# Merging TensorE's streams by estimated queues of three engines in place of constants alone

## The chip, the cores and the metric

The kernel runs on one core of a Trainium2 chip. The metric is the device time of one execution in microseconds; a lower time is better. The core has TensorE (PE in the rows, its weight loads PEld), VectorE (DVE), ScalarE (ACT), GpSimd (POOL) and SyncE (SP), which issues transfers. All five run their own instructions in order and wait for one another by semaphores.

## The reference

One inference step of a decoder trunk of two layers (`DEPTH = 2`) in float32: width 1024, a prompt of 1024 positions, and eight sample sequences with one new position each and a state of their own. A layer is, cut to what matters:

```python
p   = x @ w_in                                # q, k, v for 8 heads; r, k, v and low-rank columns for RWKV
att = dilated_attention(rope(q), rope(k), v)  # 3 patterns (window, dilation), merged per position and head
att = att * rsqrt(mean(att ** 2)) * att_gain
rw, S_T = rwkv7_time_mix(token_shift(p_rwkv), wkv0)   # delta-rule state, group norm, bonus, gate
x1  = layer_norm(ALPHA * x + concat(att, rw) @ w_out)
y   = layer_norm(ALPHA * x1 + square(relu(x1 @ w_up)) @ w_down)
```

The results are `y` for prompt and samples, the last input rows, the RWKV states and the keys and values.

## The kernel before

**Tiles.** Activations stand transposed, the 1024 features on partitions in eight tiles and positions in columns. The prompt is worked in two halves `h` of 512 columns; the second half carries the eight samples. A dense product is done to nearly float32 accuracy with three passes of a reduced format: `x` and `w` are split into a high and a low part (`xh`, `xl`, `wh`, `wl`), and `dense_steps` issues three matmuls a tile (lines 390 to 392). `Weights.fill` loads a weight piece with a DMA on ScalarE's queue, casts it on ScalarE (line 363) and subtracts on VectorE (line 364), a few pieces ahead.

**Streams.** The order of TensorE's instructions is fixed when the program is built. Seven Python generators emit the program in pieces, each up to its next `yield`:

- `dense`, the main one: `in_proj` for a layer's half, then `half(l, h)`, which is the output projection, a first normalisation, the feed-forward part in eight groups `g`, and a second normalisation;
- `s1` and `s2`, the two stages of the RWKV recurrence in units of 256 columns; `norm`, its group norm and gate (`normed`, with matmuls `pgm` and `pgv`);
- `att` (`attention`: scores `pS`, exponentials in tiles `E`, transposes `pET`, products `po` and `pof`), `post` (transposed values) and `kv` (the samples' attention).

`Streams.run` merges them by a model of time, `now`. Each step of a generator yields four things:

```python
cost, hold, lat, s[3] = r          # s[3]: the bank that its next step takes
self.now += cost                   # TensorE's own time for this step
if hold:
    self.hist[hold[0]].append(self.now + hold[1] * self.slack(s))   # the bank is free again
s[2] = self.now + lat * self.slack(s)                               # the stream can go on
```

`lat` stands for the time that the other engines need before the stream's next matmuls have their operands, and `hold` for the time until a bank of PSUM has been read. Both are constants, multiplied for side streams by `SLK`, 1.2 in a stream's first phase and 2.2 later. `run` steps the first side stream whose time has come; where none is ready, the dense stream goes on, and where that is not ready either, `now` jumps to the earliest. Four kinds of banks are shared out: `d` (3) for dense tiles, `a` (2) for most side work, `r` (1) and `o` (2) for the recurrence. `after(key, lat=...)` makes a stream wait until another has noted a key.

The tile scheduler orders the instructions of the other engines by its own model; only TensorE keeps the order in which the pieces were emitted. A matmul that stands too early in that order waits for its operand, and everything behind it on TensorE waits too.

**Where dense waits.** `half(l, h)` begins when stage two, attention and (for the second half) the samples' streams of that half are done (`Mix.wait`). In the last layer's first half this wait stands ahead of the second normalisation, at `g == LNG` (line 1000), since the next half follows at once; then `LayerNorm.start` issues the statistics matmul `lnc` (line 731).

**Constants that the change touches.** `HOLD = (2400, 4500)` is the bank time of dense tiles in the two `passes` (`out2` and `down`), in which VectorE also works on a normalisation; elsewhere it is 900. In `normed`, 900 and 1800 are the latencies ahead of `pgm` (line 1420) and `pgv` (line 1432).

Of the kernel before, what the change touches and what calls it, by code (L numbers as in the profile page):

```python
# [45 lines left out]
        "dense": (561e3, 580e3, 413e3, 427e3)}  # L46
RUN = (1600, 3200)
SWITCH = 280
HOLD = (2400, 4500)
SLK = (1.2, 2.2)  # L50
PACE = 2.0
LEAD = 0.25
# [95 lines left out]
class Streams:  # L148
# [6 lines left out]

    def __init__(self, depth):
        self.now = 0.0
        self.depth = depth  # L160
        self.hist = {b: [] for b in depth}
        self.streams = []
        self.times = {}
        self.cost = {}
        self.phase = {}
        self.work = {}
        self.stay = 0.0
        self.away = False

    def add(self, name, gen, slack=(1.0, 1.0)):  # L170
        self.streams.append([name, gen, 0.0, None, None, slack])

    def slack(self, s):
        return s[5][self.phase.get(s[0], (0,))[0] > 0]

    def note(self, *key):
        self.times[key] = self.now
# [12 lines left out]
    def ahead(self, s):  # L190

        name, main = s[0], self.streams[-1][0]
        if name not in self.work or self.phase.get(name, (0,))[0] != self.phase.get(main, (-9,))[0] + 1:
            return False
        return self.share(name) > self.share(main) * PACE + LEAD
# [14 lines left out]

    def step(self, s):
        s[3] = s[4] = None
        try:
            r = next(s[1])
        except StopIteration:
            self.streams.remove(s)
            return
        if callable(r):
            s[4] = r
            return  # L220
        cost, hold, lat, s[3] = r
        self.now += cost
        self.cost[s[0]] = self.cost.get(s[0], 0.0) + cost
        if hold:
            self.hist[hold[0]].append(self.now + hold[1] * self.slack(s))
        s[2] = self.now + lat * self.slack(s)

    def run(self):
        while self.streams:
# [34 lines left out]
    return bass.AP(tensor=ap.tensor, offset=ap.offset, ap=[list(ap.ap[0])] + [list(d) for d in dims])  # L264


@with_exitstack
def body(ctx, tc, I, O):
    nc = tc.nc
    PE, V, A, G, S = nc.tensor, nc.vector, nc.scalar, nc.gpsimd, nc.sync  # L270
    AQ = G

    cp = ctx.enter_context(tc.tile_pool(name="cp", bufs=1))
    dr = ctx.enter_context(tc.tile_pool(name="dr", bufs=1, space=DRAM))
# [6 lines left out]

    BANKS = {"r": 1, "o": 2, "d": 3, "a": 2}
    R = Streams(BANKS)
    after, note = R.after, R.note

    def bank(tag, name):
# [48 lines left out]
    class Weights:  # L335
# [4 lines left out]
        def __init__(self, specs):  # L340
            self.pieces, self.first = [], []
            for srcs, m, dest in specs:
                self.first.append(len(self.pieces))
                self.pieces += [(src, m, dest) for src in srcs]
            self.first.append(len(self.pieces))
            self.out, self.copies = {}, []
            self.nl = self.i = self.kept = 0
# [48 lines left out]
        res += pts  # L396
        res.append(cost)

    def dense(items, kts, xhh, xll, evac, hold=900):

        res = []
        yield (0, None, 0, "d")
        yield from dense_steps(items, kts, xhh, xll, res)
        for it, p in zip(items, res):
            r = evac(it, p)
            if r is not None:
                yield r
        for i, it in enumerate(items):
            yield (res[-1] if i == 0 else 0, ("d", hold + 500 * i), 0, None)

    def cols(t):
        return lambda kt, c0, n: xc(t, kt, slice(c0, c0 + n))
# [92 lines left out]
    def pv(l, nm, i):  # L505
        a = PROWS[nm][0] + i
        return par[l][0][:, a:a + 1]
# [284 lines left out]
    def acc(hs):  # L792
        return (lambda kt, c0, n: hs[kt][0][:, c0:c0 + n]), (lambda kt, c0, n: hs[kt][1][:, c0:c0 + n])
# [73 lines left out]
    def half(l, h, prev=None):  # L867
# [5 lines left out]
        if over:  # L873
# [8 lines left out]
            t = None  # L882
# [67 lines left out]
        def out2(o, w, c0, nn):  # L950
            def ev(it, p):
                _, _, c0, n = it
                evs.append(V.tensor_tensor(src(o, c0, n), p[:, :n], src(o, c0, n), op=ALU.add))
            return dense([(w, 128, c0, nn)], K4, *acc(hs), ev, HOLD[c0 > 0])
        yield from passes(out2, ln)

        def up(w, pair, c0, nn):
# [67 lines left out]
        def down(o, w, c0, nn):  # L1025
            def ev(it, p):
                _, _, c0, n = it
                to = t[:, o, c0:c0 + n]
                evs.append(V.tensor_tensor(to, p[:, :n], to, op=ALU.add))  # L1029
            return dense([(w, 128, c0, nn)], K4, *acc(hs), ev, HOLD[c0 > 0])  # L1030
        yield from passes(down, ln)

        def store(c0, n):
# [72 lines left out]
    def stage1(l, h, p, u, s, lw, out):  # L1106
# [107 lines left out]
        for hd in range(2):  # L1214
            for c in range(2):
# [2 lines left out]
                                pbs[hd].rearrange("p (b c x) -> p c b x", c=2, x=128)[:, c],  # L1218
                                bc(C("si")[:, o:o + 1], [(0, 2), (1, 128)]), op=ALU.mult)
        yield (0, ("a", 1100), 0, None)  # L1220
        d1, d2, d3 = d_el[s % 2]
        LBp = LB.rearrange("p h (b c) x -> p c (h b) x", c=2)
        for c in range(2):
# [23 lines left out]
            S.dma_start(XT[64 * c:64 * c + 64], drows(d3, c))  # L1247
        bp = tmp("sq")[:, :n]
        V.scalar_tensor_tensor(bp, zr, pv(l, "rk", p), f, op0=ALU.mult, op1=ALU.mult)
        yield (460, ("a", 1900), 0, "a")  # L1250
        tx = R.now + 30000
        pb = bank("a", "pt1")
# [162 lines left out]
    def normed(l, h, p, u, s, gup, gs):  # L1415

        y, bv = ys.pop(s)
        yield (0, None, 900, "o")
        pb = bank("o", "pgm")
        PE.matmul(pb[:, 0:256], C("blk"), y, start=True, stop=True)  # L1420
        PE.matmul(pb[:, 256:512], gup, gs[:, 0:256], start=True, stop=True)
# [2 lines left out]
        A.copy(gg, pb[:, 256:512])  # L1424
        sq = rq.tile([128, 4, 128], F32, tag="FG", name="gq").rearrange("p a b -> p (a b)")[:, 0:256]
        A.activation(sq, y, AF.Square)
        yield (860, ("o", 1000), 1800, "o")
        pb = bank("o", "pgv")
        if h == 1 and u == NU - 1:
            PE.matmul(pb[:, 256:256 + NB], gup, gs[:, UN:UN + NB], start=True, stop=True)  # L1430
# [149 lines left out]
    def attention(l, h, p, ops, vT, ahead):  # L1580
# [5 lines left out]
        for j in range(4):  # L1586
# [29 lines left out]
            for hd in range(2):  # L1616
# [13 lines left out]
                V.reciprocal(mx[:, 8 + hd:9 + hd], mx[:, 6 + hd:7 + hd])  # L1630
                V.tensor_scalar(E[:, :f + w], E[:, :f + w], mx[:, 8 + hd:9 + hd], None, op0=ALU.mult)
            if j == 3:
                ahead()
            yield (0, None, ALT0 + (f + w) * ALT1, "a")
            if h == 1 and j % 2 == 0:
                FT = ap_.tile([128, 2, 4, 2, 32], F32, tag="FT", name="FT")
# [277 lines left out]
```

## Time and profile before

| | |
|---|---|
| median of 3 runs | 3244.0 us (3242.94 to 3245.74) |
| profiled execution, its own time | 3244.69 us |
| its span, first to last instruction | 3242.9 us |
| TensorE matmuls busy | 3054.3 us, 94% |
| VectorE, ScalarE, GpSimd busy | 63%, 44%, 29% |
| mean granted TensorE clock | 0.974 of full |

The busy times are those of one profiled execution; idle time of TensorE is the span less its busy time. A matmul's end is modelled, so a busy TensorE is not one at its peak. In a list of waits, `PE pgm L1420 <- ACT y L1401` says that TensorE sat idle before the matmul into `pgm` of line 1420 until ScalarE's instruction on `y` of line 1401 had ended.

### The profile page before, as it was taken

How to read it: one execution, taken by the hardware profiler on the slowest of the kernel's cores; microseconds unless marked ns; L12 is line 12 of the kernel's file. 1: busy time of each engine (PE TensorE's matmuls, PEld its weight loads, DVE VectorE, ACT ScalarE, POOL GpSimd, SP SyncE). 2: the span in 40 equal slices, each digit the busy share in tenths (PEclk: the TensorE clock that was granted, in tenths of full speed). 3: DMA queues.
4: the chain of work that ended last, by engine and by line, in shares of the span. 5: the costliest groups of instructions: out<-in, count | busy, mean ns of one | idle time of the engine just before them, and what ended most of it. 6: DMA issues, size and time to landing. Idle time of an engine off the chain costs nothing. (4 is left out here: it accounts for less than half of the span.)

```text
span 3242.9 us, 66797 instructions
## 1 busy us (share of the span) xinstructions
PE 3054.3 (94%) x25212; PEld 2651.7 (82%) x25212; DVE 2034.9 (63%) x4671; ACT 1439.2 (44%) x3266; POOL 930.1 (29%) x1761
## 2 busy tenths in 40 slices
PE   9999999899989999989999999888999999899998
PEld 6778887777767887778899999877777777889997
DVE  5666666865575575677565566467755754965556
ACT  4446444453433363455443345344543333543333
POOL 1444435532310214453310112545242201400011
PEclk9999999999999999989999999999999999999999
DMA  7445455344343355533233236544343433422332
GB/s 233 144 128 143 132 144 164 88 129 122 105 134 103 98 157 156 163 101 105 85 91 97 89 94 183 142 134 124 104 131 108 121 123 105 137 81 93 93 91 82
DMA packets 370506, 393.64 MB, mean 121 GB/s; under 512 B 145816, under 2 KB 223080, under 8 KB 370184
## 3 DMA queue, kind: packets, MB, share of 16 engines
q10 hardware_dynamic: 121152, 213.44, 22.0%
q1 hardware_dynamic: 249032, 175.93, 19.1%
q8 instruction: 199, 3.26, 0.4%
q14 instruction: 123, 1.01, 0.1%
HBM read 325.30 MB, written 63.97 MB: 120 GB/s over the span
## 5 line engine op out<-in xcount | busy, mean ns | idle before, releaser
L390 PE MATMUL dps<-xh,wh 128*128 128x256 f32 (+3 forms) x2984 | 976.0, 327 | 11.4 <-ACT wh L363 6.6
L391 PE MATMUL dps<-xl,wh 128*128 128x256 f32 (+3 forms) x2984 | 950.6, 319 | 14.7 <-DVE xl L782 11.9
L392 PE MATMUL dps<-xh,wl 128*128 128x256 f32 (+3 forms) x2984 | 945.8, 317 | 0.2 <-DVE u L550 0.2
L363 ACT CAST wh<-wr 128x512 fp32r<-128x512 f32 (+1 forms) x772 | 475.0, 616 | 825.5 <-PE dps L391 759.9
L364 DVE TENSOR_TENSOR wl<-wr,wh 128x512 fp32r<-128x512 f32 (+1 forms) x772 | 578.4, 750 | 414.7 <-ACT wh L363 394.8
L390 PEld LDWEIGHTS dps<-xh,wh 128*128 128x128 f32 x2984 | 570.5, 191 | 68.3 <-issue 13.6
L391 PEld LDWEIGHTS dps<-xl,wh 128*128 128x128 f32 x2984 | 570.5, 191 | 53.6 <-DVE xl L782 18.0
L392 PEld LDWEIGHTS dps<-xh,wl 128*128 128x128 f32 x2984 | 569.7, 191 | 38.3 <-DVE wl L364 0.8
L390 PE MATMUL dps<-hh,wh 128*128 128x512 f32 (+2 forms) x1600 | 525.2, 328 | 7.2 <-DVE hh L964 5.1
L391 PE MATMUL dps<-hl,wh 128*128 128x512 f32 (+2 forms) x1600 | 514.9, 322 | 3.0 <-DVE hl L965 1.9
L392 PE MATMUL dps<-hh,wl 128*128 128x512 f32 (+2 forms) x1600 | 513.5, 321 | 0.0
L390 PEld LDWEIGHTS dps<-hh,wh 128*128 128x128 f32 x1600 | 305.0, 191 | 39.5 <-issue 8.2
L391 PEld LDWEIGHTS dps<-hl,wh 128*128 128x128 f32 x1600 | 305.1, 191 | 25.4 <-DVE hl L965 2.6
L392 PEld LDWEIGHTS dps<-hh,wl 128*128 128x128 f32 x1600 | 304.9, 191 | 22.7
L1235 POOL TENSOR_TENSOR tm<-BL,XB 32x15 f32<-32x15 f32 (+7 forms) x480 | 156.1, 325 | 386.0 <-DMA BL<-d_el 297.2
L996 DVE TENSOR_TENSOR t<-dps,t 128x256 f32<-128x256 f32 (+1 forms) x240 | 123.8, 516 | 158.2 <-PE dps L392 157.4
L749 POOL TENSOR_TENSOR ln<-ln,lsq 128x256 f32<-128x256 f32 (+1 forms) x112 | 92.7, 828 | 287.8 <-ACT lsq L747 285.5
L1237 POOL TENSOR_TENSOR XB<-XB,tm 32x15 f32<-32x15 f32 (+7 forms) x480 | 154.1, 321 | 33.8
L738 POOL TENSOR_TENSOR t<-t,ln 128x256 f32<-128x256 f32 (+1 forms) x32 | 28.1, 915 | 394.6 <-ACT ln L732 394.6
L964 DVE CAST hh<-rl 128x256 fp32r<-128x256 f32 (+2 forms) x200 | 72.0, 360 | 108.7 <-ACT rl L963 105.7
L738 POOL TENSOR_TENSOR t<-t,lnm 128x256 f32<-128x256 f32 (+1 forms) x80 | 69.6, 903 | 245.6 <-ACT lnm L732 230.7
L962 ACT ACTIVATE rl<-dps 128x256 f32<-128x256 f32 (+2 forms) x200 | 88.4, 442 | 111.3 <-PE dps L392 102.1
(347 smaller groups left out, 5012.5 us busy)
## 6 DMA issues: line engine op xcount, KB each, us to landing
wr<-in_w_ff_up ACTq DMA_DIRECT2D x272, 256.0 KB
wr<-in_w_ff_down ACTq DMA_DIRECT2D x256, 256.0 KB
wr<-in_w_in ACTq DMA_DIRECT2D x220, 256.0 KB
stg<-d_qkv SPq DMA_DIRECT2D x128, 128.0 KB
wr<-in_w_out ACTq DMA_DIRECT2D x64, 256.0 KB
z<-d_z SPq DMA_DIRECT2D x24, 384.0 KB
d_qkv<-qe SPq DMA_DIRECT2D x128, 64.0 KB
kvc<-in_cache_k SPq DMA_DIRECT2D x32, 256.0 KB
```

Source lines behind the costliest of these rows:

```text
L363: self.copies.append(A.copy(h[:, :, :m], w[:, :, :m]))
L364: V.tensor_tensor(lo[:, :, :m], w[:, :, :m], h.bitcast(F32)[:, :, :m], op=ALU.subtract)
L390: PE.matmul(p[:m, :n], wh[:, wk % 4, :m], hi, start=(i == 0), stop=False)
L391: PE.matmul(p[:m, :n], wh[:, wk % 4, :m], lo, start=False, stop=False)
L392: PE.matmul(p[:m, :n], wl[:, wk % 4, :m], hi, start=False, stop=(i == last))
L738: G.tensor_tensor(t, t, self.cm[:, c0:c0 + n], op=ALU.subtract)
L749: G.tensor_tensor(s2, s2, sq, op=ALU.add)
L962: A.activation(r, p[:, :n], AF.Relu)
L964: V.tensor_copy(hh[:, c0:c0 + n], r)
L996: V.tensor_tensor(to, p[:, :n], to, op=ALU.add)
L1235: G.tensor_tensor(tv, bc(BL[:, 17 * j + 1:17 * j + 2], [(1, m), (0, j + 1)]), bc(XB[:, 16 * j:16 * j + 1], [(0, m), (1, j + 1)]), op=ALU.mult)
L1237: G.tensor_tensor(xv, xv, tv, op=ALU.add)
```

## The change

`Streams` gets a queue for each of VectorE, ScalarE and GpSimd. A wrapper `Engine` stands in for the three engines: each call is priced by a fixed list (a base and a time per element, for one or for two large operands; a DMA issue 340 ns) and added to that engine's queue, from the model's `now` or the queue's end, whichever is later. `behind` is the latest end among what one step has issued. A bank is then free at the later of the constant's time and `behind`, and a stream whose `lat` is over 0 goes on at the later of the constant's time and `behind + 400`. `HOLD` is dropped (all dense tiles 900). Two latencies of `normed` become 1500 and 2400. In two places `behind` is saved and put back, so that what is issued between (the block inversion on GpSimd, the prefetch of the next attention operands) doesn't delay its own stream, though it stays in the queues. No instruction is added or removed.

```diff
-HOLD = (2400, 4500)
...
+        self.queue = {}
+        self.behind = 0.0
...
+    def busy(self, name, t):
+
+        self.queue[name] = max(self.queue.get(name, 0.0), self.now) + t
+        self.behind = max(self.behind, self.queue[name])
...
     def step(self, s):
         s[3] = s[4] = None
+        self.behind = 0.0
...
         if hold:
-            self.hist[hold[0]].append(self.now + hold[1] * self.slack(s))
+            self.hist[hold[0]].append(max(self.now + hold[1] * self.slack(s), self.behind))
         s[2] = self.now + lat * self.slack(s)
+        if lat > 0:
+            s[2] = max(s[2], self.behind + 400)
...
+class Engine:
+
+    COST = {"V": (155, 0.55, 1.04), "A": (215, 0.78, 0.78), "G": (110, 1.4, 2.8)}
...
+        def call(*args, **kw):
+            base, one, two = self.COST[self.name]
+            if op == "dma_start":
+                t = 340
+            else:
+                aps = [a for a in list(args) + [kw.get("in0"), kw.get("in1")] if hasattr(a, "shape") and len(a.shape) > 1]
+                if not aps:
+                    return f(*args, **kw)
+                n = math.prod(aps[0].shape[1:])
+                big = [a for a in aps[1:] if math.prod(a.shape[1:]) >= n > 1]
+                t = base + n * (two if len(big) > 1 else one)
+            self.streams.busy(self.name, t)
+            return f(*args, **kw)
...
     R = Streams(BANKS)
+    V, A, G = Engine(V, "V", R), Engine(A, "A", R), Engine(G, "G", R)
+    AQ = G
...
-            yield (res[-1] if i == 0 else 0, ("d", hold + 500 * i), 0, None)
+            yield (res[-1] if i == 0 else 0, ("d", 900 + 500 * i), 0, None)
...
         yield (0, ("a", 1100), 0, None)
+        behind = R.behind
         d1, d2, d3 = d_el[s % 2]
...
         V.scalar_tensor_tensor(bp, zr, pv(l, "rk", p), f, op0=ALU.mult, op1=ALU.mult)
+        R.behind = behind
...
-        yield (0, None, 900, "o")
+        yield (0, None, 1500, "o")
...
-        yield (860, ("o", 1000), 1800, "o")
+        yield (860, ("o", 1000), 2400, "o")
...
             if j == 3:
+                behind = R.behind
                 ahead()
+                R.behind = behind
```

## Rows read from the trace of the kernel before

**Rows 1.** TensorE's busy time, share of the span and instructions, the page's part 1.

```profile
PE 3054.3 (94%) x25212; PEld 2651.7 (82%) x25212; DVE 2034.9 (63%) x4671; ACT 1439.2 (44%) x3266; POOL 930.1 (29%) x1761
```

**Rows 2.** Windows by stage: length; busy time of each engine; granted clock, DMA.

```profile
60.00:480.00 420.00, 393.81 (x3826) 333.92 (x3824) 265.34 (x692) 204.66 (x505) 187.34 (x409) 0.98 0.49 139
480.00:1040.00 560.00, 526.19 (x4436) 423.89 (x4429) 367.03 (x863) 242.52 (x563) 179.70 (x344) 0.97 0.42 122
...
1200.00:1735.00 535.00, 506.30 (x4475) 440.56 (x4475) 337.68 (x820) 254.20 (x596) 181.17 (x369) 0.96 0.40 117
...
2040.00:2692.00 652.00, 607.10 (x5047) 491.85 (x5047) 411.90 (x973) 280.17 (x653) 206.99 (x400) 0.96 0.41 120
```

**Rows 3.** TensorE's waits: who waited for whom, us in total, times, longest us.

```profile
PE pgm L1420 <- ACT y L1401: 11.1, 9, 2.3
PE pET L1641 <- DVE E L1631: 8.8, 3, 6.5
PE pgv L1432 <- ACT gq L1426: 8.7, 3, 4.5
PE pO L1389 <- DVE Z L1396: 8.5, 8, 2.0
...
PE pPQ L1349 <- DVE XT L1341: 7.3, 5, 3.8
PE pn L1171 <- ACT sg L570: 6.9, 4, 5.7
...
PE pgv L1432 <- DVE gsd L1431: 5.6, 5, 3.3
...
PE pqt L698 <- DVE mx L1624: 4.8, 2, 2.5
...
PE pof L1673 <- ACT FT L1657: 4.3, 1, 4.3
PE pS L1619 <- DVE ao L1666: 4.1, 1, 4.1
...
PE pX L1309 <- ACT T L1331: 3.2, 3, 1.5
...
PE pO L1389 <- DVE u L552: 2.5, 1, 2.5
```

**Rows 4.** Groups by line, shapes apart, VectorE, ScalarE, GpSimd: times, busy, mean ns.

```profile
L364 DVE TENSOR_TENSOR wl<-wr,wh 128x512 fp32r<-128x512 f32 x764 | 574.9, 753 | 409.7 <-ACT wh L363 390.0 <-DMA kvc<-in_cache_v 2.4 <-DMA d_qkv<-qe 2.3
...
L363 ACT CAST wh<-wr 128x512 fp32r<-128x512 f32 x764 | 472.7, 619 | 821.7 <-PE dps L391 757.2 <-DMA wr<-in_w_in 29.8 <-DMA wr<-in_w_ff_up 10.5
...
L1562 POOL TENSOR_SCALAR qf<-stg 128x512 f32<-128x512 f32 x8 | 16.9, 2110 | 25.1 <-PE pS L1603 16.8 <-DMA stg<-d_qkv 8.3
```

**Rows 5.** Windows: a normalised pass with side streams.

```profile
2251.00:2285.00 34.00, 25.12 (x247) 21.89 (x246) 25.99 (x74) 17.66 (x49) 7.05 (x8) 0.85 0.21 63
```

**Rows 6.** Windows before and after 2215 us; the clock stands ahead of the DMA share.

```profile
2211.00:2215.00 4.00, 0.34 (x2) 0.00 (x0) 4.00 (x3) 0.62 (x1) 3.16 (x5) 0.93 0.00 0
2215.00:2221.00 6.00, 5.88 (x37) 4.95 (x38) 4.66 (x11) 1.87 (x4) 1.79 (x2) 0.50 0.39 132
```

**Rows 7.** Timeline about 2207 us: start us, us, instructions.

```profile
2206.82 7.89 DVE L853 TENSOR_TENSOR hl<-am,hh 128x512 fp32r<-128x512 f32 x1
...
2207.28 6.88 POOL L738 TENSOR_TENSOR t<-t,lnm 128x256 f32<-128x256 f32 x10
```

**Rows 8.** VectorE's line 853: duration ns min/median/max.

```profile
L853 DVE TENSOR_TENSOR hl<-am,hh x16: 673/698/7892, 569.7 to 2803.2; 128x512 fp32r<-128x512 f32 x8, 128x520 fp32r<-128x520 f32 x8
```

**Rows 9.** Timeline of TensorE ahead of the gate in half (1, 0).

```profile
2669.16 0.39 PE L1620 MATMUL pS<-kS,qL 128*128 128x512 f32 x1
...
2680.49 1.04 PE L1641 MATMUL pET<-cst,E 128*128 128x128 f32 x8
...
2690.54 0.69 PE L1673 MATMUL pof<-FT,vT 128*64 128x64 f32 x16
...
2691.95 1.03 PE L731 MATMUL lnc<-t,onec 128*128 128x256 f32 x4
```

## What was predicted before the changed kernel was run

> **What bounds the kernel now.** I read the page first: TensorE's matmuls cover 3054.3 of 3242.9 us [rows 1], so TensorE is the path and at most 188.6 us of idle time can go, plus what its clock costs. No instruction is added or taken away by this change; TensorE gets the same 25,212 matmuls in another order. So I asked next in which stages the idle time lies. In the four stretches in which side streams run between dense tiles, TensorE is idle for 26.2, 33.8, 28.7 and 44.9 us, 134 us together, and the granted clock is 0.98, 0.97, 0.96 and 0.96 [rows 2]. In those stretches the clock costs 0.02 x 420 + 0.03 x 560 + 0.04 x 535 + 0.04 x 652 = 73 us at full rate. The other 55 us of idle time lie at the start, at the end and where the dense stream is alone; there no other stream is ready, so no rule of merging can fill them.
>
> Then the list of TensorE's waits, which names who ended each. Its side-stream rows [rows 3] are what the change aims at: a side matmul stands in TensorE's order before its operand is there, and all dense work behind it waits too. Two things are to be seen. Many waits are of 1 to 2 us, so small errors of the model's latencies make them; and they end on DVE or ACT, hardly on a DMA. VectorE is busy for 411.9 of 652 us in the last merged stretch [rows 2], so an operation there often stands behind others.
>
> **The change, part by part.** *The price list.* It charges a 512-element two-operand VectorE operation 155 + 1.04 x 512 = 687 ns, a ScalarE cast of 512 elements 614 ns and a GpSimd copy of 512 elements 827 ns; the trace has means of 753, 619 and 2110 ns [rows 4]. The first two are near enough to follow a queue; GpSimd's strided copies are not, but none of TensorE's larger waits ends on GpSimd [rows 3], so I cost that error at nothing.
>
> *The norm stream's constants* (900 to 1500, 1800 to 2400, times a slack of 1.2 in the first phase and 2.2 after it). Each of the two waits gets 0.72 or 1.32 us more. The present waits are 11.1 us in 9 (ending on y), 8.7 us in 3 (gq) and 5.6 us in 5 (gsd) [rows 3]. The nine have a mean of 1.2 us, so about 9 go; the three lose 1.3 each, 4; the five, of 1.1 us mean, lose 5. Sum -18. Bounds: -8, if half of the added time is eaten because the operand is late for another cause, and -25, all of them. Two later starts a unit make the norm chain about 2.6 us longer; what hides it is that stage two's next unit runs meanwhile.
>
> *Waits for VectorE.* With the estimated queue a side stream's next step starts no sooner than 400 ns after the last operation it issued, and a bank is free no sooner than its reader. The rows for Z 8.5, XT 7.3, ao 4.1, mx 4.8, u 2.5 and E 8.8 us [rows 3] are such. I take two out: the longest on E, 6.5 us, because the attention step already waits (2500 + 4 x 512) x 2.2 = 10 us, more than I expect the estimated queue to be; and the longest on XT, 3.8 us, for a reason below. Left are 8.5 + 3.5 + 4.1 + 4.8 + 2.5 + 2.3 = 25.7 us. In these the operand is late by a microsecond or so after a queue of several operations, but the model's queue is in order of emission and starts an operation at its step's begin, while the real order of VectorE is set by the tile scheduler. I take half, -13; bounds 0 and -36.
>
> *Waits for ACT.* The rows for sg 6.9, FT 4.3 and T 3.2 us [rows 3] make 14.4. ScalarE is busy for 280.2 of 652 us [rows 2], so its queue is short and it is late mostly because it waits itself, which the model doesn't follow. I take -6; bounds 0 and -14.
>
> *HOLD.* The fixed bank times of 2400 and 4500 ns in the normalised passes go; the estimated queue of VectorE takes their place. In such a pass with side streams VectorE is busy for 26.0 of 34 us and TensorE for 25.1 [rows 5]; there are three of them. Eight tiles of 1420 ns of matmuls stand against VectorE's sums, scalings and evictions of more than that, so the estimated queue grows and holds dense back about as long. I cost it at 0; bounds -10 and +27 (as much idle time again in each of three). Where no side stream is left, nothing can be put in between and the order stays.
>
> *The parts that set the queue aside* (prefetch of attention operands, the block inversion on GpSimd) keep those long chains from delaying their own stream. But the casts of a prefetch stay in ACT's queue, some 4 to 6 x 614 ns, and delay the next steps of all side streams in the model though the chip would run others first. This costs nothing while a stream has room before its due time; where it has none, see the second rival.
>
> *The clock.* In the 4 us before 2215 us TensorE works for 0.34 us at a granted clock of 0.93; in the 6 us after it, it works for 5.88 us and the clock is 0.50, that is 1.2 in place of 2.4 GHz [rows 6]. Fewer gaps mean fewer such stretches. Idle time won is 18 + 13 + 6 = 37 us of 134, that is 0.28 of 73 us, -20. Bounds 0 and -40.
>
> *What comes back.* A later side step doesn't vanish: it lands behind other dense tiles and meets other queues, and the new order moves the issues of SP and ACT too. No row shows that order. Below, nothing comes back; above, all of it does. I take half of 57, +28, since the rows show that waits are spread thinly over a dozen places [rows 3] rather than in one.
>
> Sum: -18 - 13 - 6 + 0 - 20 + 28 = -29 us. The profiled execution took 3244.7 us in all, 1.8 more than its span, and the median of the runs is 3244.0, so the two can be taken as one. Forecast **3216 us**, 0.9% faster.
>
> **A lock that the queues don't know.** One VectorE subtraction took 7.89 us beside a run of ten GpSimd operations that took 6.88 us together [rows 7]; the median of its line is 698 ns [rows 8]. TensorE's longest wait on XT, 3.8 us, stands right behind it, which is why I left it out above. The Trainium skill (SBUF — State Buffer, "SBUF: two separate sides") says that VectorE and GpSimd share a port pair under an exclusive lock, and that a VectorE operation with two SBUF inputs blocks fully against a GpSimd operation that reads SBUF. The trace agrees in this place, 7.89 against 0.70 us. By that rule a sum of fixed prices misses the longest delays of VectorE.
>
> As a mechanism of this kernel: if nothing of the waits for VectorE is caught, -18 and -6 stay, 24 of 134 us, the clock gives 0.18 x 73 = 13, and half of 37 comes back: -19 us, 3226 us. It lies inside the forecast's own range, and I give it 0.12 of that case's chance.
>
> **The rivals.** *No change.* The estimated queue is nearly always shorter than the slacked constant, so the maximum keeps the old number; or the delays come from operations that run far over their price, as the one of 7.89 us [rows 7]. Then only the norm stream's constants act, -18 and about -10 of clock, and a new order gives as much back: 3244 us. For it speaks that an attention step's 10 us and stage two's 1500 x 2.2 = 3.3 us are long against prices of 0.4 to 0.7 us; against it, that waits on VectorE outlast these very constants [rows 3].
>
> *Slower, by the gate before the second normalisation of half (1, 0).* There the dense stream waits until attention and stage two of half (1, 1) are done. Attention's last matmul starts at 2690.54 us and the dense stream's next step behind the gate at 2691.95 us, with three dense matmuls between [rows 9]: the room is about 1 us. If attention's steps come later against the dense work, dense runs dry at the gate, and TensorE has only what is left of attention, a short burst in each 10 to 20 us. Against it: the step from the last score matmul (2669.16) to the transposes (2680.49) takes 11.3 us [rows 9], as the model's (2500 + 4 x 640) x 2.2 = 11.1 us has it, and an estimated queue under that changes nothing. For it: the prefetch casts in ACT's queue and the banks that now stay taken until the queue's end. The chain has 16 steps of this kind. Each microsecond late at the gate costs about one; the rival decides from 29 + 6.5 = 36 us late, 2.2 us a step. At 4 us a step, 64 us late: 3216 + 64 = 3280 us.
>
> **How the numbers follow.** Within 0.2% means 6.5 us either way, about what a measurement of this kernel can tell from no change. Forecast case 0.60, its own range 3170 to 3237 (all caught is -25 - 36 - 14 - 40 = -115; a third of it back gives 3168, and the upper end is -0.2%). No change 0.15. Gate 0.17. The forecast's mechanism with more coming back than was won, at the upper bounds of what comes back and of HOLD, 3244.7 + 27 = 3272 us: 0.08. So faster 0.60, same 0.15, slower 0.25. The range takes in the gate's case up to some 55 us late: 3165 to 3270.
>
> **What would show it.** Right: the norm rows pgm and pgv fall from 25.4 to under 10 us; the waits of Z, mx and ao halve; idle time of the four merged stretches falls from 134 to near 110 us, the clock there rises by about 0.005 to 0.01; the stretches of dense work alone keep their length. Wrong: the side rows keep their sum under other names (no change); a stretch in the last merged stage with few dense matmuls and an idle TensorE just before the statistics matmul of the second normalisation (gate); idle time over 9 us in the pass of [rows 5] (HOLD). Most of all the forecast fails if the new order makes new waits as fast as it removes old ones, which nothing in a profile of the old order can tell.

## The result, and the profile after

The changed kernel takes 3262.33 us (median of 4 runs, 3258.31 to 3266.54) where the kernel before takes 3243.98 (4 runs, 3242.94 to 3245.74): a ratio of 1.0056 of the means, 95% interval 1.0043 to 1.0068. It is slower by 0.56%. A gain of 0.9% was forecast. The time lies inside the range given, on the wrong side of no change.

The profiled execution took 3261.86 us, with a span of 3260.1 us. Part 1 of its page answers to [rows 1]:

```profile
PE 3073.0 (94%) x25212; PEld 2663.8 (82%) x25212; DVE 2029.7 (62%) x4671; ACT 1437.4 (44%) x3266; POOL 923.2 (28%) x1761
```

TensorE's idle time is 3260.1 - 3073.0 = 187.1 us; before it was 188.6. So between these two executions it did not grow. The same 25,212 matmuls were busy for 18.7 us longer, and that is the whole difference of the two. The mean granted clock fell from 0.974 to 0.969. The span times what is missing from the full clock is 0.026 x 3242.9 = 84 us before and 0.031 x 3260.1 = 101 us after, so some 17 of the 18.7 us are the clock's.

Two single executions can mislead here, since the clock of one kernel differs from run to run. In its four runs the changed kernel had 0.968 to 0.972, with a mean of 0.970. The kernel before had 0.967 to 0.977, with a mean of 0.972, in the 114 runs beside the experiments below; its profile, at 0.974, is better than that mean. How much of the loss is the clock's is taken up again under "All taken together".

The stretches with side streams, at the same stage marks, answer to [rows 2] (length, busy time of each engine, granted clock, DMA share and GB/s):

```profile
60.00:488.00 428.00, 399.51 (x3686) 337.50 (x3685) 253.86 (x678) 203.68 (x500) 184.82 (x402) 0.95 0.47 134
488.00:1050.00 562.00, 534.23 (x4577) 427.80 (x4575) 364.94 (x878) 245.93 (x571) 177.49 (x352) 0.97 0.42 122
...
1210.00:1746.00 536.00, 506.53 (x4468) 442.49 (x4467) 342.57 (x820) 250.16 (x592) 184.77 (x367) 0.97 0.40 115
...
2050.00:2708.00 658.00, 608.68 (x5042) 492.27 (x5042) 419.93 (x975) 278.85 (x653) 201.77 (x399) 0.96 0.41 119
```

TensorE is idle in them for 28.5, 27.8, 29.5 and 49.3 us, 135 in all, against 134 before. To place the loss without choosing marks by eye, I cut both traces where a normalisation's statistics matmul `lnc` starts. First the kernel before:

```profile
60.00:571.00 511.00, 478.69 (x4647) 406.67 (x4645) 326.06 (x833) 248.08 (x605) 242.80 (x504) 0.98 0.50 143
571.00:1056.00 485.00, 457.31 (x3678) 364.16 (x3678) 313.41 (x734) 202.63 (x470) 124.24 (x249) 0.97 0.40 114
1056.00:1394.00 338.00, 318.47 (x2033) 263.88 (x2032) 203.19 (x421) 161.33 (x348) 110.34 (x195) 0.96 0.49 145
1394.00:1848.00 454.00, 436.48 (x4173) 407.80 (x4174) 283.37 (x701) 200.96 (x472) 101.99 (x221) 0.97 0.32 92
1848.00:2204.00 356.00, 333.23 (x2891) 309.81 (x2890) 224.11 (x509) 167.67 (x386) 132.44 (x230) 0.96 0.48 139
2204.00:2692.00 488.00, 460.89 (x3636) 362.99 (x3636) 313.82 (x737) 207.66 (x478) 128.63 (x248) 0.97 0.39 114
```

The same windows of the kernel after:

```profile
60.00:582.00 522.00, 486.62 (x4611) 412.96 (x4610) 317.88 (x828) 244.71 (x594) 225.98 (x470) 0.95 0.48 140
582.00:1066.00 484.00, 463.12 (x3719) 365.34 (x3719) 308.16 (x739) 208.10 (x482) 136.34 (x284) 0.97 0.39 114
1066.00:1402.00 336.00, 317.69 (x2016) 262.98 (x2014) 204.54 (x413) 160.31 (x345) 114.52 (x195) 0.96 0.48 144
1402.00:1857.00 455.00, 436.96 (x4189) 409.29 (x4190) 285.32 (x708) 199.64 (x475) 102.03 (x221) 0.98 0.33 94
1857.00:2215.00 358.00, 331.25 (x2895) 308.44 (x2894) 228.45 (x509) 168.66 (x386) 130.57 (x230) 0.97 0.47 138
2215.00:2707.00 492.00, 463.74 (x3635) 364.44 (x3635) 316.74 (x737) 206.07 (x478) 124.47 (x248) 0.96 0.39 114
```

The lengths differ by +11, -1, -2, +1, +2 and +4 us, and the rest by +2. Eleven of 17 us lie in the first stage, where TensorE is busy 8 us longer with 36 matmuls fewer: the clock there is 0.95 in place of 0.98.

What a short wait can be followed by is seen at 133 us. Windows about it (the clock stands before the DMA share), and TensorE's timeline:

```profile
129.00:131.00 2.00, 1.46 (x13) 0.86 (x11) 1.05 (x2) 0.59 (x1) 0.00 (x0) 1.00 0.57 175
131.00:133.00 2.00, 1.21 (x7) 1.00 (x8) 1.44 (x6) 0.00 (x0) 0.00 (x0) 1.00 0.69 202
133.00:147.00 14.00, 12.35 (x67) 8.98 (x68) 5.95 (x14) 6.40 (x20) 3.50 (x4) 0.51 0.38 113
```

```profile
124.69 0.39 PE L432 MATMUL dps<-xh,wl 128*128 128x512 f32 x1
124.92 0.39 PE L430 MATMUL dps<-xh,wh 128*128 128x512 f32 x1
...
131.79 0.44 PE L1661 MATMUL pS<-kS,qS 128*128 128x384 f32 x1 [1.33 <-DVE ao L302]
...
135.06 0.63 PE L431 MATMUL dps<-xl,wh 128*128 128x512 f32 x1
135.48 0.63 PE L432 MATMUL dps<-xh,wl 128*128 128x512 f32 x1
```

A score matmul waits 1.33 us for `ao`, between small side matmuls of three streams; it is TensorE's only listed wait from 118 to 135 us. From 133 to 147 us the granted clock is 0.51, that is 1.2 GHz for nearly all of it; dense matmuls start 0.42 us apart where they started 0.23 us apart. The 12.35 busy us cost an estimated 12.35 x 0.49 = 6 us, four to five times the wait ahead of them. In the same 40 us (120 to 160) of the kernel before, the clock is 1.00. In [rows 6] a pause of nearly 4 us was followed by 6 us at half clock, and in the changed kernel TensorE is idle for 5.1 us from 240 to 260 us at a granted clock of 0.83, which is some 7 us at half clock. So the length of a gap doesn't tell the clock's price; that the place of a gap does is argued from this one case. (Lines of this kernel are shifted, and instructions of VectorE, ScalarE and GpSimd all have line 302, that of the wrapper; go by tiles.)

TensorE's waits (us in total, times, longest us) answer to [rows 3]:

```profile
PE dps L431 <- DVE xl L302: 14.6, 28, 1.3
PE pn L1211 <- ACT sg L302: 14.0, 7, 6.0
PE pO L1431 <- DVE Z L302: 11.1, 9, 4.0
PE pT L1351 <- DMA X<-d_el: 10.6, 11, 1.9
PE dps L430 <- DVE ln L302: 10.4, 7, 2.4
PE pT L1351 <- DVE XT L302: 8.7, 5, 4.2
PE pgv L1474 <- DVE gsd L302: 8.0, 8, 4.1
...
PE pgm L1462 <- ACT y L302: 7.0, 4, 3.7
PE pgv L1474 <- ACT gq L302: 6.3, 3, 3.0
...
PE pPQ L1391 <- DVE XT L302: 5.8, 3, 3.4
PE pqt L738 <- DVE mx L302: 3.9, 1, 3.9
...
PE pX L1351 <- ACT T L302: 3.3, 2, 2.9
...
PE pS L1661 <- DVE ao L302: 2.0, 2, 1.3
...
PE pET L1685 <- DVE E L302: 1.0, 1, 1.0
```

The twelve rows of [rows 3] had 75.8 us; the same twelve now have 62.4 (those on `FT` and `u` are gone). Others grew: `pT` on `XT`, which had no row before, to 8.7, `pT` on the transfer of `X` from 8.0 to 10.6, dense on `xl` from 11.9 to 14.6 and on `ln` from 8.0 to 10.4.

### The profile page after: what moved, and what is told of

It reads as the page before. It is cut to its first block, busy times and chain, and to the rows that moved or that the text cites. A ratio compares the mean times of both kernels' runs of the same rounds, so it can differ in the third digit from the quotient of the medians.

```text
span 3260.1 us, 66768 instructions
## 1 busy us (share of the span) xinstructions
PE 3073.0 (94%) x25212; PEld 2663.8 (82%) x25212; DVE 2029.7 (62%) x4671; ACT 1437.4 (44%) x3266; POOL 923.2 (28%) x1761
## 4 chain that ended last, share of the span: by engine, by line
PE 42%; DVE 8%; DMA 5%; POOL 3%; issue 2%; ACT 2%; SPq 1%; ACTq 0%; DVEq 0%; POOLq 0%
PE dps L430 12%; PE dps L431 12%; PE dps L432 12%; DVE t L302 2%; DVE wl L302 1%; DMA wr<-in_w_out 1%; DVE xl L302 1%; DVE ln L302 1%; POOL XB L302 1%; POOL tm L302 1%; DMA d_el<-LB 1%; DMA sq<-d_z 1%; PE po L1708 1%; DVE hl L302 0%; PE pX L1351 0%
## 5 line engine op out<-in xcount | busy, mean ns | idle before, releaser
L431 PE MATMUL dps<-xl,wh 128*128 128x256 f32 (+3 forms) x2984 | 955.1, 320 | 16.9 <-DVE xl L302 14.6
L430 PE MATMUL dps<-hh,wh 128*128 128x512 f32 (+2 forms) x1600 | 524.8, 328 | 10.5 <-DVE t L302 4.7
L302 DVE TENSOR_TENSOR t<-dps,t 128x256 f32<-128x256 f32 (+2 forms) x352 | 169.8, 484 | 189.0 <-PE dps L432 184.7
L302 POOL TENSOR_TENSOR t<-t,lnm 128x256 f32<-128x256 f32 (+1 forms) x80 | 67.3, 874 | 207.8 <-ACT lnm L302 199.3
```

Source lines behind the costliest of these rows:

```text
L302: return f(*args, **kw)
L430: PE.matmul(p[:m, :n], wh[:, wk % 4, :m], hi, start=(i == 0), stop=False)
L431: PE.matmul(p[:m, :n], wh[:, wk % 4, :m], lo, start=False, stop=False)
```

## The experiments

All eighteen kernels were timed beside the kernel before on the same chip; ratios are to that. Five chips were used, on which the kernel before has medians of 3247.9 to 3252.5 us. The table is referred to below by labels (us; idle is span less TensorE's busy time, of the one profiled execution; the row of the kernel before is that of the profile above):

| kernel | ratio, 95% interval | span | TensorE busy | idle |
|---|---|---|---|---|
| before | 1 | 3242.9 | 3054.3 | 188.6 |
| after | 1.0056 [1.0043, 1.0068] | 3260.1 | 3073.0 | 187.1 |
| e1 | 1.0039 [1.0024, 1.0054] | 3257.8 | 3060.9 | 196.9 |
| e2 | 1.0018 [0.9998, 1.0038] | 3264.2 | 3064.3 | 199.9 |
| e3 | 0.9937 [0.9911, 0.9963] | 3234.0 | 3061.1 | 172.9 |
| e4 | 0.9973 [0.9959, 0.9986] | 3246.3 | 3047.0 | 199.3 |
| e5 | 1.0004 [0.9988, 1.0019] | 3250.2 | 3055.0 | 195.2 |
| e6 | 1.0043 [1.0031, 1.0055] | 3259.5 | 3070.2 | 189.3 |
| e7 | 0.9948 [0.9930, 0.9966] | 3233.4 | 3056.0 | 177.4 |
| e8 | 1.0059 [1.0036, 1.0081] | 3261.3 | 3057.9 | 203.4 |
| e9 | 1.0000 [0.9986, 1.0013] | 3248.6 | 3056.0 | 192.6 |
| e10 | 0.9908 [0.9886, 0.9929] | 3221.8 | 3046.9 | 174.9 |
| e11 | 1.0000 [0.9990, 1.0010] | 3241.4 | 3060.2 | 181.2 |
| e12 | 0.9978 [0.9966, 0.9990] | 3243.6 | 3053.1 | 190.5 |
| e13 | 1.0023 [1.0012, 1.0034] | 3253.3 | 3066.9 | 186.4 |
| e14 | 1.0051 [1.0031, 1.0071] | 3257.2 | 3064.0 | 193.2 |
| e15 | 0.9931 [0.9907, 0.9955] | 3227.5 | 3051.2 | 176.3 |
| e16 | 0.9995 [0.9982, 1.0008] | 3244.6 | 3052.8 | 191.8 |
| e17 | 0.9998 [0.9982, 1.0015] | 3250.8 | 3066.7 | 184.1 |
| e18 | 0.9983 [0.9970, 0.9997] | 3247.4 | 3060.1 | 187.3 |

The theory at the start: one part of the change carries the loss. Its rival: any new order makes about as many new gaps as it removes, and the sign is chance.

**Parts taken apart, e1 to e4.** e1 is the kernel before with the two constants of `normed` alone; e2 to e4 are the changed kernel without one or both of the two queue rules.

```diff
# e1, in the kernel before
-        yield (0, None, 900, "o")
+        yield (0, None, 1500, "o")
...
-        yield (860, ("o", 1000), 1800, "o")
+        yield (860, ("o", 1000), 2400, "o")
# e2 and e3, in the changed kernel: the bank rule off
-            self.hist[hold[0]].append(max(self.now + hold[1] * self.slack(s), self.behind))
+            self.hist[hold[0]].append(self.now + hold[1] * self.slack(s))
# e2 and e4: the readiness rule off
-            s[2] = max(s[2], self.behind + 400)
+            pass
```

> The kernel before with the two norm latencies of the change alone (1500 and 2400). If the estimated queues make the loss (theory), the constants alone take a part of the 25 us of waits before pgm and pgv and the time is 3225 to 3242 us. If the constants make it (rival 1), 3255 us or more. If any new order moves the time at random by about half a per cent (rival 2), anywhere from 3225 to 3265 us, whatever becomes of the waits before pgm and pgv.

> The changed kernel with both queue rules taken out: norm latencies 1500 and 2400, all dense tiles at 900, no HOLD. Theory: 3225 to 3245 us, with TensorE's clock at 0.973 or more. Rival 1 (constants or the loss of HOLD): 3255 to 3265 us and a clock of 0.970 or less. Against the run with the norm constants alone it shows what HOLD is worth; I expect under 5 us.

> The changed kernel with the rule for when a stream goes on, without the rule for when a bank is free. Theory: this rule holds side steps back and bunches them, so it carries most of the loss: 3252 to 3265 us, clock loss in the first 480 us as in the changed kernel (half clock for 40 us or more of them). Rival 1: 3255 to 3265 us too, and the same with the bank rule alone. Rival 2: no relation to the changed kernel.

> The changed kernel with the rule for when a bank is free, without the rule for when a stream goes on. Theory: 3230 to 3250 us, half clock for under 30 us of the first 480 us. Rival 1: 3255 to 3265 us. Rival 2: no relation to the changed kernel.

Measured 1.0039, 1.0018, 0.9937 and 0.9973. The readiness rule with the new constants (e3) gains 0.6%, and each rule beside the constants is faster than neither; both together are slower than all three. The parts don't add. The theory for e3, that this rule carries most of the loss (3252 to 3265 us), was wrong: 3235.1. From e1 to e2 only `HOLD` goes, without a queue in its place: 1.0039 to 1.0018, with intervals that overlap. e1 is the most telling. Its waits:

```profile
PE pT L1309 <- DMA X<-d_el: 23.7, 9, 11.7
PE pn L1171 <- ACT sg L570: 15.1, 8, 5.8
...
PE pgv L1432 <- DVE gsd L1431: 8.8, 8, 2.5
...
PE pgv L1432 <- ACT gq L1426: 5.7, 3, 3.0
...
PE pgm L1420 <- ACT y L1401: 3.1, 4, 1.3
```

The norm rows fall from 25.4 us [rows 3] to 17.6, so the constants do what they say; but `pT` now waits 23.7 us for `X` (8.0 before, the line below) and `pn` 15.1 for `sg` (6.9), and idle time is 8.3 us above that of the kernel before (another chip). What was won came back more than once.

```profile
PE pT L1309 <- DMA X<-d_el: 8.0, 5, 4.0
```

**Each rule alone, and how much an order's luck is worth, e5 to e8.** e7 and e8 add one rule alone to the kernel before, with its old constants and `HOLD`. e5 and e6 are controls, small edits that change the order and bring no knowledge of queues.

```diff
# e5, in the kernel before: the model's cost of going back to dense
-SWITCH = 280
+SWITCH = 290
# e6, in the changed kernel
-            s[2] = max(s[2], self.behind + 400)
+            s[2] = max(s[2], self.behind + 450)
# e7 (e8: the other max alone), in the kernel before, with Engine and busy
+        if lat > 0:
+            s[2] = max(s[2], self.behind + 400)
```

> A control: the kernel before, with SWITCH 290 in place of 280 model ns, an edit that says nothing about queues and gives another order. If the parts of the change have values of their own (theory A), a control stays within 0.15% of the kernel before. If any new order moves the time by half a per cent either way (theory B), it can be off by 0.3% or more.

> A control: the changed kernel with behind + 450 in place of behind + 400. Theory A: as the changed kernel, 0.4 to 0.7% over the kernel before. Theory B: anywhere from 0.6% under to 0.8% over it.

> The kernel before plus the rule for when a stream goes on, nothing else (HOLD and the norm latencies 900 and 1800 as before, no bank rule). Theory A: this rule is worth about what it gave with the new constants, 0.4 to 0.9% faster than the kernel before, TensorE's idle time under 165 us. Theory B: no sign to be told ahead.

> The kernel before plus the rule for when a bank is free, nothing else. Theory A: alone it does little, within 0.3% of the kernel before. Theory B: no sign to be told ahead.

Measured 1.0004, 1.0043, 0.9948 and 1.0059. The readiness rule is a gain with either set of constants (0.9937, 0.9948). The bank rule alone is a loss here, where theory A had it within 0.3%; with the new constants it was 0.9973 (e4). e7's idle time, 177.4 us, misses the 165 that its first answer asked for. The controls e5 and e6 stay within 0.15% of the kernels that they were made from.

**Where the bank rule acts, e9 to e12.** e9 is both rules with the old constants and `HOLD`. e10 has the bank rule on dense tiles alone, e11 on the side banks alone; e12 is a control without queues that moves most side steps.

```diff
# e10, in the changed kernel (e11: hold[0] != "d")
-            self.hist[hold[0]].append(max(self.now + hold[1] * self.slack(s), self.behind))
+            self.hist[hold[0]].append(max(self.now + hold[1] * self.slack(s), self.behind * (hold[0] == "d")))
# e12, in the kernel before
-SLK = (1.2, 2.2)
+SLK = (1.3, 2.4)
```

> The kernel before plus both queue rules, with HOLD and the norm latencies of before. It closes the table of lat rule, bank rule and constants. Theory A (the lat rule wins 0.5 to 0.6%, the bank rule loses as much or more on top of it): 0.2 to 0.8% slower than the kernel before. If the two rules simply add: within 0.2% of it (0.9948 x 1.0059 = 1.0007). If HOLD's loss is what turns the pair bad: 0.3% or more faster.

> The changed kernel with the bank rule for the dense tiles' banks alone. If it loses by holding dense tiles back, so that side steps follow each other without dense work between (theory A1): 0.3% or more slower than the kernel before, as the changed kernel. If the loss is in the side streams' banks (theory A2): 0.3 to 0.8% faster, as with the lat rule alone.

> The changed kernel with the bank rule for the side streams' banks alone, not for dense tiles. Theory A1: 0.3 to 0.8% faster than the kernel before. Theory A2 (a bank with one or two buffers that is held to the queue's end sets the pace of the side chain and bunches its steps): 0.3% or more slower.

> The kernel before with SLK (1.3, 2.4) in place of (1.2, 2.2): every side step a tenth later, no queue. If the lat rule wins only because it makes side steps later (rival), this wins too: 0.3% or more faster, idle time under 168 us. If it wins because it makes those later that meet a queue, this stays within 0.3% of the kernel before or loses.

Measured 1.0000, 0.9908, 1.0000 and 0.9978. e10 is the fastest kernel found. Turning the bank rule off on the side banks takes the change from +0.6% to -0.9%. Turning it off on the dense tiles takes it to 0.0% (e11), which fits neither answer. e9 is the case in which the two rules simply add. e12 wins 0.2% with idle time at 190.5 us, so later side steps without a queue bring less than half of what the readiness rule brings.

**Which bank, and why, e13 to e16.** e13 counts only operations that read a bank in the bank rule, to test whether it loses because it holds a bank until everything that a step issued has ended. e14 and e15 put the rule on `d` and `a`, and on all but `a`. e16 is a control of e10.

```diff
# e13, in the changed kernel; reads: an input of the call lies in a bank of PSUM
+        if reads:
+            self.read = max(self.read, self.queue[name])
...
-            self.hist[hold[0]].append(max(self.now + hold[1] * self.slack(s), self.behind))
+            self.hist[hold[0]].append(max(self.now + hold[1] * self.slack(s), self.read))
# e14 and e15, like e10
+            self.hist[hold[0]].append(max(self.now + hold[1] * self.slack(s), self.behind * (hold[0] in "da")))
+            self.hist[hold[0]].append(max(self.now + hold[1] * self.slack(s), self.behind * (hold[0] in "dro")))
# e16, in e10
-            s[2] = max(s[2], self.behind + 400)
+            s[2] = max(s[2], self.behind + 450)
```

> The changed kernel with a bank held until the estimated end of the last operation of the step that reads a bank, in place of the last operation of any kind. If the side banks cost because the rule counts operations that come after the reading (theory A2a), 0.5 to 1.0% faster than the kernel before, like the rule on dense tiles alone. If holding side banks to a queue's end is harmful in itself (A2b), 0.2% or more slower. If it is the spread of any order (B), between.

> The changed kernel with the bank rule for the banks d and a, not for r and o. If the two banks of a, which attention, stage one and four others share, carry the loss: 0.3% or more slower than the kernel before. If r and o of the recurrence carry it: 0.5% or more faster.

> The changed kernel with the bank rule for d, r and o, not for a. If a carries the loss: 0.5% or more faster than the kernel before; if r and o do: 0.3% or more slower.

> A control around the fastest order so far (lat rule, and bank rule for dense tiles alone): behind + 450 in place of + 400. If its 0.9% is the work of the rules: 0.7 to 1.1% faster than the kernel before. If half of it is the luck of one order: 0.2 to 0.7%.

Measured 1.0023, 1.0051, 0.9931 and 0.9995. e13 is better than the change by 0.3% and worse than e10 by far, so the operations behind a bank's reading are at most a small part. e14 against e15 points at the `a` banks, which most side streams share. But e16 is a warning, and gains less than either of its answers said: 50 ns more in one rule cost e10 0.9%. The windows from 60 us on to `lnc` marks place the 30 us between e14 and e15; first e14, then e15:

```profile
60.00:581.00 521.00, 484.21 (x4609) 411.58 (x4608) 320.08 (x828) 244.66 (x594) 226.39 (x470) 0.96 0.50 140
581.00:1069.00 488.00, 464.99 (x3720) 366.61 (x3720) 308.62 (x740) 208.22 (x482) 136.14 (x284) 0.97 0.40 113
```

```profile
60.00:567.00 507.00, 473.93 (x4603) 402.02 (x4603) 315.05 (x825) 243.47 (x592) 224.66 (x469) 0.98 0.50 143
567.00:1044.00 477.00, 458.57 (x3718) 363.95 (x3717) 310.50 (x741) 206.02 (x482) 133.62 (x284) 0.98 0.41 116
```

Twenty-five of the 30 us lie in these two stages, and of these 16.7 are busy time at a lower clock (949.2 against 932.5 us for 8 matmuls more). The change has most of its own loss in the first of these stages too, at a clock of 0.95.

**The last two, e17 and e18.** The rule on `a` alone, and e15 with the edit of e16.

```diff
# e17, in the changed kernel
+            self.hist[hold[0]].append(max(self.now + hold[1] * self.slack(s), self.behind * (hold[0] == "a")))
# e18, in e15
-            s[2] = max(s[2], self.behind + 400)
+            s[2] = max(s[2], self.behind + 450)
```

> The changed kernel with the bank rule on the two a banks only, the readiness rule and the constants kept. If the rule on the a banks carries the loss, the ratio is that of the kernels that had it so far, 1.000 to 1.006; if those ratios were only the luck of one order, it lies as likely by the mean of the kernels without it, 0.994 (0.991 to 0.9995). A value of 0.997 to 1.000 tells neither apart.

> The changed kernel with the bank rule on d, r and o but not on a, and 450 in place of 400 in the readiness rule: a control of the 0.993 without that edit. If leaving the a banks out is the gain, it stays under 0.998; if 0.993 was the luck of one order, it comes to 1.000 or over.

Measured 0.9998 and 0.9983; both fall between the two answers.

**All taken together.** Thirteen kernels have the readiness rule. In the six without the bank rule on `a` (e3, e7, e10, e15, e16, e18) the ratios are 0.9908 to 0.9995, mean 0.9950; in the seven with it (after, e6, e9, e11, e13, e14, e17) 0.9998 to 1.0056, mean 1.0024. The two sets don't overlap, but the gap between them is only 0.0003, and a change of 50 ns or of another bank moves the ratio by up to 0.9% within the first set and 0.6% within the second. Four pairs differ in the rule on `a` and in nothing else: e3 and e17, e10 and e14, e15 and after, e18 and e6. In each the kernel with the rule is slower, by 0.6, 1.4, 1.3 and 0.6%, and the two intervals don't overlap. The place is the same, too. In the eleven kernels with the readiness rule and the new constants, the first `lnc` starts at 579.5 to 584.5 us where `a` has the rule (six) and at 564.0 to 572.1 where it has not (five). That the rule on `a` costs some 0.7% on the mean beside the readiness rule and the new constants is likely, then. It is not a price of the rule by itself: with the old constants the first `lnc` starts at 575.6 us without it (e7) and 572.1 with it (e9), and e4, which has it without the readiness rule, starts it at 560.9 and is faster than the kernel before. Nor does this start decide the time by itself: e5, as fast as the kernel before, has 586.4. The two groups differ by 7.6 us of idle time (187.7 against 180.1) and 10.6 us of busy time (3065.3 against 3054.7). By which steps the rule does so stays open: e13 shows that the operations behind the reading are not most of it.

How much of this is the clock's can be estimated over all runs of a kernel, since each has its span and clock on record: span x (1 - clock) is the part short of the full clock (a little too much, as idle time at half clock is in it), and the rest is everything else. Against the kernel before on the same chip, e6, which is the change but for 50 ns, is 13.9 us longer, 5.5 by the clock and 8.4 by the rest; e14 is 14.7 longer (8.4 and 6.2), e1 13.7 (0.7 and 12.9), e15 24.3 shorter (10.5 and 13.8), e10 27.6 shorter (13.6 and 14.0). So over many runs the clock's part goes from next to nothing (e1) to four fifths (e7, 11.7 of 14.7 us shorter), and in the change's near copy it is two fifths, where the two profiles of the change gave nearly all.

Attention's products end at another place, too. The rows of `pof` (ns min/median/max, first and last start), e14 and then e15:

```profile
L1717 PE MATMUL pof<-FT,vT x256: 219/222/270, 490.0 to 2697.9; 128*64 128x64 f32 x128
```

```profile
L1717 PE MATMUL pof<-FT,vT x256: 219/222/270, 477.4 to 2637.5; 128*64 128x64 f32 x128
```

With `a` held, attention ends 60 us later, just ahead of the gate. Still, in the change the stage from 2204 us on holds only 4 of the 17 us, as shown next.

## Why the prediction was wrong

Two steps failed: what comes back was put too low, and the clock was given a gain where it brought a loss. Which of them is the larger the runs don't settle. Term by term:

*What bounds the kernel* held: TensorE is the path, and the difference of the two spans is that of its busy and idle time.

*The norm constants*, -18 (bounds -8 to -25): alone -7.8 us in their own rows (e1), in the change -4.1 (25.4 to 21.3). The sign asked for was under 10 us. The five waits on `gsd` became eight, in e1 as in the change; why is not shown. The mechanism is right, the size half and less.

*Waits for VectorE*, -13: the rows on `E`, `Z`, `XT`, `ao`, `mx` and `u` fell from 36.0 to 23.8 us, -12.2, though by other rows than argued: the longest on `E`, which I had taken out of the sum as one that stays, went, and `Z` rose. The total is right by luck. *Waits for ACT*, -6: from 14.4 to 17.3 us, +2.9. The text's own doubt, that ScalarE is late because it waits itself, fits, but no run tests it.

*HOLD*, 0 (bounds -10 to +27): the three passes before, of which [rows 5] shows the third, and after:

```profile
614.00:646.00 32.00, 25.52 (x218) 21.57 (x215) 26.42 (x70) 14.85 (x39) 16.07 (x37) 0.89 0.19 48
1435.00:1470.00 35.00, 30.92 (x276) 25.74 (x275) 30.05 (x78) 21.43 (x55) 9.22 (x12) 0.85 0.16 44
```

```profile
627.00:647.00 20.00, 18.96 (x197) 17.24 (x195) 19.89 (x52) 11.52 (x31) 7.91 (x7) 1.00 0.16 37
1440.00:1465.00 25.00, 19.65 (x156) 16.44 (x158) 24.21 (x57) 15.52 (x44) 14.11 (x26) 1.00 0.18 47
2267.00:2291.00 24.00, 20.80 (x204) 17.94 (x204) 23.96 (x61) 12.68 (x35) 6.26 (x7) 0.98 0.13 38
```

TensorE was idle in them for 6.5 + 4.1 + 8.9 = 19.5 us and now for 1.0 + 5.4 + 3.2 = 9.6, at a clock near 1.00 in place of 0.85 to 0.89. That is the lower bound, -10. But the passes hold fewer side matmuls now (741 matmuls of all kinds in the three before, 557 after; the pass's own are the same), and these run elsewhere.

*What comes back*, "I take half": of the 13.4 us that left the rows of [rows 3], 11.9 came back, since idle time fell by 1.5 only. In e1 more came back than went, most of it on the transfer of `X`, a row that the prediction passed over when it read that waits end hardly on a DMA. Half was too little. It is no rule that all comes back: e3 and e7 keep idle times of 172.9 and 177.4 us.

*The clock*, -20, has the wrong sign: "Fewer gaps mean fewer such stretches", with the loss in proportion to idle time. Between the two profiles idle time went by -1.5 us and busy time by +18.7, and no term of the sum could turn a new order into a loss of clock. At 133 us a gap of 1.33 us among small side matmuls was followed by 6 us of lost clock. Against the forecast of 3216, idle time accounts for some 17 us of the miss by these two profiles (-18.5 forecast, that is -37 with half back; -1.5 measured) and the clock for 29 (-10 with half back; +18.7). By the ten runs of e6 it is the other way round: some 16 us by the clock (+5.5) and 27 by the rest (+8.4).

Is the proportion itself wrong? In the twenty single executions of the table idle time runs from 172.9 to 203.4 us and busy time from 3046.9 to 3073.0, with a correlation of 0.06; e4 has nearly the most idle time and the second lowest busy time. But single executions carry the spread of the clock from run to run. Over all runs of the eighteen experiments, each against the kernel before on its chip, the clock's part and the rest have a correlation of 0.56. So orders that lose less elsewhere do tend to lose less clock, as the prediction had it; for one order it decides little (e4 gains 8.6 us of clock and loses 1.9 of the rest).

*The lock.* The same subtraction again took 7.9 us in one of 16, as in [rows 8]:

```profile
L302 DVE TENSOR_TENSOR hl<-am,hh x16: 679/690/7897, 579.5 to 2818.6; 128x512 fp32r<-128x512 f32 x8, 128x520 fp32r<-128x520 f32 x8
```

The queues don't know of it, and it did not change. The rule of the Trainium skill cited above (SBUF — State Buffer, "SBUF: two separate sides") agrees with 7.897 against 0.690 us, and no run here took the GpSimd work beside it away.

*The rivals.* No change is out, by the interval. The gate is out: the last attention matmuls and the gate's `lnc` after,

```profile
2698.68 0.69 PE L1717 MATMUL pof<-FT,vT 128*64 128x64 f32 x16
...
2707.03 1.02 PE L771 MATMUL lnc<-t,onec 128*128 128x256 f32 x4
```

are 8.3 us apart with TensorE full of dense work between, where [rows 9] had 1.4; and the stage that ends there is longer by 4 us, of which 2.9 are busy time. The fourth, "more coming back than was won" (3272 us, 0.08), comes nearest, though its price is not that of HOLD, and in the two profiles it is the clock's. My last sentence, that new waits may come as fast as old ones go, was the right doubt with too small a chance.

The aim of the change holds as far as idle time goes. Four pairs differ in the readiness rule alone (before and e7, e2 and e3, e4 and after, e8 and e9), and with it the idle time of the profiled execution is lower by 11.2, 27.0, 12.2 and 10.8 us. The time is lower in three of them (by 0.5, 0.8 and 0.6%) and higher by 0.8% in the one that leads to the change. The bank rule beside it, probably that on `a`, gave the gain away: from e3 to the change it costs 1.2%.

## What to carry to other kernels

Where a merge order is planned by a model, don't forecast a new order from the waits of the old one alone. Count what the aimed-at rows can lose, assume that most of it can come back elsewhere, and give the clock a term of both signs (here 14 us better to 8 worse than the kernel before, over all runs). Read a difference of clock from many runs and not from one profile of each. Test a planner's rule in its parts, in pairs that differ in it alone, and beside controls that reorder without knowing more; a single order says little when an edit of 50 ns can be worth 0.9%. Look at what follows a short gap among small matmuls, too, and not only at the long ones.

## What the runs showed of the hardware

The same program doesn't get the same clock each time. The kernel before ran in 3239.12 to 3265.57 us with a granted clock of 0.967 to 0.977, in 114 runs on five chips. A change of 0.005 in the clock of two single executions, as between 0.974 and 0.969 here, is within that spread. The profiles of e11 and e17 have 0.974 and 0.970, but the means of their ten runs are 0.973 and 0.972. So the span of a single profiled execution can be off by some 10 us, and the single rows of the table are to be read with that in mind.

A gap's length doesn't set what it costs in clock: in the changed kernel 1.33 us idle was followed by 14 us at 0.51 of the clock, and in the kernel before a pause of nearly 4 us was followed by 6 us at 0.50 [rows 6].
